# The resident tiles of an encoder kernel laid out in another order, with every large tile at a multiple of 512 bytes

## The chip, the core and the metric

The kernel runs on one core of a Trainium2 chip, in one launch. The metric is the device time of one execution in microseconds. Each core has a matrix engine (TensorE, PE in the profile, with its weight loads listed apart as PEld), a vector engine (VectorE, DVE), a scalar engine (ScalarE, ACT), a general one (GpSimd, POOL) and a queue engine (SyncE, SP). The on-chip memory SBUF has 128 partitions; a tile takes the same bytes in each partition, so its place is one number, the byte at which it starts. Matmuls read both operands from SBUF and write to PSUM.

## The reference

One layer of an encoder trunk on 1024 tokens of width 1024, all in float32:

```python
h = x
hn = rmsnorm(h, norm_mix_g)
z = hn @ w_in                               # 1024 x 2048
u, (q, k, v) = z[..., :512], split(z[..., 512:], 3)
a = pool_mixer(u, pool_w, pool_b, pool_scale)
o = chunk_attention(q, k, v, rel_bias)      # 8 heads, own chunk of 64 and 8 before it
h = h + concat([a, o]) @ w_out
hn = rmsnorm(h, norm_ffn_g)
gt, val = split(hn @ w_up, 2)               # 1024 x 2816 each
gt = causal_dwconv(gt, conv_w, conv_b)      # width 3
h = h + (gelu(gt) * val) @ w_down
gate = sigmoid(rmsnorm(h, norm_ple_g) @ w_ple_gate + b_ple_gate)
h = h + gate * (p @ w_ple)
return rmsnorm(h, final_g)
```

## The kernel before

Matmul operands are split in two parts, a rounded high one and the rest (`split`, lines 132 to 134: ScalarE writes the high part, VectorE the low one), and each product is three matmuls into one PSUM bank (`mm3`, lines 126 to 130):

```python
pe.matmul(ps, ahi, bhi, start=first, stop=False, skip_group_check=more)
pe.matmul(ps, ahi, blo, start=False, stop=False, skip_group_check=more)
pe.matmul(ps, alo, bhi, start=False, stop=last, skip_group_check=more)
```

The second operand named is the stationary one (the weights, 128 columns), the third the moving one (512 columns in most places, 256 or 320 in the attention and in the last token groups). Each matmul has a weight load of its own, which the profile shows as LDWEIGHTS under the same line.

Everything that stays on chip lies in a few large tiles, allocated once at the head of `trunk` (lines 103 to 111), which the rest of the kernel cuts up by offset. `R` (128 KiB per partition) holds operands in the matmul's number format, `F` holds plain float32 data. `ident` is the unit matrix for transposes; `vec` holds gains, biases and convolution weights by column (136 words); `small` holds statistics, counts and a column of ones (80 words). Behind these, a second region is used by one tile after another, each for a stage: `B` (attention and output projection: half of the weight ring, the probabilities, V's weights), then `V` and `TB`, `B3` (first gated products and weights of the down projection), `BQ` and `RW`, `B3T`, and `B4` (the last projection). `r(kb, n)` and `f(kb, n)` give slices of R and F at `kb` KiB; `r` with kb from 128 up goes to B.

The tiles are packed in the order in which the pool names them. The first free byte of a partition is 1152, behind 1024 bytes of DMA scratch and four constants at 32 bytes each. So the places before are

| tile | bytes | starts at | modulo 512 |
|---|---|---|---|
| R | 131072 | 1152 | 128 |
| F | 62464 | 132224 | 128 |
| ident | 512 | 194688 | 128 |
| vec | 544 | 195200 | 128 |
| small | 320 | 195744 | 160 |
| B, V, B4 | 32768, 4096, 32768 | 196064 | 480 |
| TB, B3, BQ, B3T | up to 28672 | 200160 | 480 |
| RW | 16384 | 212448 | 480 |

Nearly all operands in R and the B tiles are at multiples of 512 bytes from the start of their tile.

The stages, in order of time: norm, first projections and V (to about 50 us); attention with the other projections filled in between its steps (to about 280 us); pooling mix and output projection; then the feed-forward part. That one works on 22 blocks of 128 hidden units. `up` makes a block's two up products from seven half-size products (`step`, line 784, and `product`, line 728), whose weights are summed by GpSimd and split ahead by `prepare`, three steps before their use. The first two blocks go down by `down` (lines 861 to 876) out of `B3`. The sixteen blocks 2 to 17 go down in four groups by seven half-size products each (`down_next`, lines 980 to 994), called in between the steps of `up`; its four operand pairs lie in three quarters of `BQ` and, the fourth, at `r(60)`:

```python
spots = [B[:, 1024 * z:1024 * (z + 1)] for z in range(3)] + [r(60, 1024)]
```

The first two of them are weights, the third and the fourth moving operands. One call has 24 matmuls: four output tiles by two pairs by three. Each call then splits the next operands out of `RW`, into which SP's and GpSimd's queues load and add the stored blocks `Yd` and the weights. Blocks 18 and 19 go down out of `B3T`, in whose products one of six weight slices lies in R (again `r(60)`), the last two out of R. `ple_mm` and `gate_mm` (lines 1122 to 1134) are the last projections.

TensorE's order is written out by hand, as the code runs; the other engines are ordered by the recording layer. [...]

Of the kernel before, what the change touches and what calls it, by code (L numbers as in the profile page):

```python
# [6 lines left out]
F32 = mybir.dt.float32  # L7
# [4 lines left out]
P = 128  # L12
# [26 lines left out]
NVEC = C_GL + KT  # L39
# [54 lines left out]
def trunk(tc, xT, pT, vecs, w_qk0, w_in, w_v, bias, counts, pool_w, w_out, w_up, w_down,  # L94
# [4 lines left out]
    with tc.tile_pool(name="sb", bufs=1) as sb, \  # L99
            tc.tile_pool(name="ps", bufs=1, space=bass.MemoryType.PSUM) as pp, \  # L100
            tc.manual_schedule(engines={mybir.EngineType.PE}):

        R = sb.tile([P, 32768], F32R, name="R")
        F = sb.tile([P, 15616], F32, name="F")
        ident = sb.tile([P, P], F32, name="ident")
        vec = sb.tile([P, NVEC], F32, name="vec")
        small = sb.tile([P, 80], F32, name="small")
        PS = pp.tile([P, 8, 512], F32, name="PS")

        b_pool = tc.tile_pool(name="b1", bufs=1)  # L110
# [4 lines left out]
        def r(kb, n):  # L115
            if kb >= 128:
                return B[:, int((kb - 128) * KW):int((kb - 128) * KW) + n]
            return R[:, int(kb * KW):int(kb * KW) + n]

        def f(kb, n):  # L120
            return F[:, int(kb * KW):int(kb * KW) + n]

# [1154 lines left out]
```

## Time and profile before

| | |
|---|---|
| time, median of 3 runs | 1167.14 us (1165.75 to 1167.91) |
| span of the profiled execution | 1166.0 us |
| granted TensorE clock, mean of the span | 0.997 |
| DMA traffic | 115.93 MB, mean 99 GB/s |
| matmuls and weight loads | 5747 each |

The profile is of one execution. Its span runs from the first to the last instruction. A line of a group view gives line, engine, operation, written tile <- read tiles, shape, count, then busy time and mean of one in ns, then the engine's idle time just before them and what ended it. For PEld the names are those of the matmul that the load belongs to: "PS<-R" has both operands in R, "PS<-BQ" both in BQ, "PS<-R,BQ" one in each. A line of the order of time gives start, length, engine, line, operation and operands. Matmuls are pipelined, so their bars overlap: what one costs in a dense stretch is the distance between two starts, its pitch.

### The profile page before, as it was taken

The page shows a single profiled execution, that of the slowest core. Times are in us where ns is not written, and L with a number is a line of the kernel's source. Part 1 is how long each engine was busy: PE and PEld are TensorE (multiplying, and loading weights), DVE is VectorE, ACT ScalarE, POOL GpSimd, SP SyncE. Part 2 cuts the span into 40 slices and gives each one's busy share as a digit, 9 for nine tenths or more (in the row PEclk, how much of TensorE's full clock was granted, in tenths as well). Part 3 has the DMA queues.
Part 4 walks back from the last instruction along what each step waited for, and adds up shares of the span by engine and source line. Part 5 has one row for each costly group of instructions (what it writes and reads, how often), then busy time and mean ns, then how long its engine had stood idle before and what let it go on. Part 6 is the DMA issues. An engine that isn't in the chain of part 4 may idle for free.

```text
span 1166.0 us, 15841 instructions
## 1 busy us (share of the span) xinstructions
PE 1142.9 (98%) x5747; PEld 962.3 (83%) x5747; DVE 926.7 (79%) x1462; ACT 569.2 (49%) x991; POOL 290.1 (25%) x267
## 2 busy tenths in 40 slices
PE   9999999999999999999999999999999999999997
PEld 7988998888888778778788888887888877888897
DVE  7678877879557797889889898988898899885543
ACT  8568687665555541333343343433344345544433
POOL 0000000082003431333533353335233422120000
PEclk9999999999999999999999999999999999999999
DMA  7110102115400121544754585567556912510012
GB/s 260 37 48 30 49 12 67 40 27 182 135 27 2 55 73 38 143 127 126 167 149 127 154 176 140 128 161 167 141 133 157 207 28 91 179 47 1 1 73 73
DMA packets 58974, 115.93 MB, mean 99 GB/s; under 512 B 6672, under 2 KB 7952, under 8 KB 58896
## 3 DMA queue, kind: packets, MB, share of 16 engines
q1 hardware_dynamic: 47232, 93.88, 25.0%
q0 software_dynamic: 11520, 20.98, 11.0%
q8 instruction: 45, 0.74, 0.3%
q14 instruction: 33, 0.27, 0.1%
q10 hardware_dynamic: 144, 0.07, 0.0%
HBM read 101.79 MB, written 13.11 MB: 99 GB/s over the span
## 4 chain that ended last, share of the span: by engine, by line
PE 75%; DVE 9%; issue 7%; DMA 3%; ACT 3%; POOL 2%; SPq 0%; POOLq 0%; DVEq 0%; ACTq 0%
PE PS L129 23%; PE PS L128 23%; PE PS L130 22%; DVE R L134 3%; PE PS L367 2%; DMA RW<-Yd 1%; PE PS L384 1%; PE PS L385 1%; DMA F<-in_w_up 1%; POOL F L700 1%; POOL RW L945 1%; PE PS L342 1%; PE PS L341 1%; DVE V L805 1%; ACT R L133 1%
## 5 line engine op out<-in xcount | busy, mean ns | idle before, releaser
L128 PE MATMUL PS<-R 128*128 128x512 f32 (+1 forms) x1144 | 431.2, 377 | 8.2 <-ACT F L782 3.1
L130 PE MATMUL PS<-R 128*128 128x512 f32 (+1 forms) x1144 | 426.5, 373 | 0.9 <-DVE R L134 0.9
L129 PE MATMUL PS<-R 128*128 128x512 f32 (+1 forms) x1080 | 408.0, 378 | 0.3 <-DVE R L230 0.3
L128 PEld LDWEIGHTS PS<-R 128*128 128x128 f32 x1144 | 215.8, 189 | 47.8 <-ACT F L782 4.3
L130 PEld LDWEIGHTS PS<-R 128*128 128x128 f32 x1144 | 215.6, 188 | 40.4 <-DVE R L134 2.4
L133 ACT ACTIVATE R<-F 128x512 fp32r<-128x512 f32 (+2 forms) x217 | 136.0, 638 | 203.9 <-PE PS L129 137.1
L129 PEld LDWEIGHTS PS<-R 128*128 128x128 f32 x1080 | 203.9, 189 | 36.5 <-DVE R L230 1.1
L700 POOL TENSOR_TENSOR F<-F 128x512 f32<-128x512 f32 x88 | 154.9, 1760 | 275.2 <-DVE R L134 166.3
L134 DVE TENSOR_TENSOR R<-F,R 128x512 fp32r<-128x512 f32 (+2 forms) x213 | 171.2, 809 | 29.4 <-ACT R L133 28.3
L992 DVE TENSOR_TENSOR F<-F,PS 128x512 f32<-128x512 f32 x112 | 73.2, 678 | 8.6 <-PE PS L130 8.0
L133 ACT ACTIVATE BQ<-RW 128x512 fp32r<-128x512 f32 x72 | 42.0, 622 | 58.3 <-PE PS L129 55.2
L945 POOL DMA_DIRECT2D RW<-Yd x48 | 44.5, 927 | 102.9 <-DMA RW<-Yd 60.8
L609 ACT ACTIVATE F<-F 128x512 f32<-128x512 f32 (+1 forms) x49 | 27.9, 570 | 56.4 <-DVE F L1143 28.0
L353 ACT ACTIVATE F<-F,small 128x640 f32<-128x640 f32 (+2 forms) x64 | 44.4, 693 | 21.1 <-DVE small L351 13.0
L134 DVE TENSOR_TENSOR BQ<-RW,BQ 128x512 fp32r<-128x512 f32 x72 | 52.2, 756 | 3.1 <-PE PS L129 2.7
L375 DVE TENSOR_TENSOR B<-PS,B 128x640 fp32r<-128x640 f32 (+2 forms) x64 | 41.9, 655 | 9.9 <-ACT B L374 8.9
L819 ACT ACTIVATE F<-F,vec 128x1024 f32<-128x1024 f32 (+1 forms) x24 | 28.2, 1174 | 42.4 <-DVE F L801 41.4
L322 POOL MEMSET F<- 64x64 f32 x8 | 1.2, 152 | 183.6 <-ACT F L321 157.6
L129 PE MATMUL PS<-BQ 128*128 128x512 f32 x112 | 44.6, 398 | 1.5 <-DVE BQ L134 1.5
L129 PE MATMUL PS<-R,BQ 128*128 128x512 f32 x112 | 45.0, 402 | 0.3 <-DVE R L134 0.3
L374 ACT ACTIVATE B<-PS 128x640 fp32r<-128x640 f32 (+2 forms) x64 | 35.9, 561 | 17.7 <-PE PS L367 14.9
L130 PE MATMUL PS<-BQ 128*128 128x512 f32 x112 | 44.4, 397 | 0.0
(195 smaller groups left out, 2090.7 us busy)
## 6 DMA issues: line engine op xcount, KB each, us to landing
F<-in_w_up SPq DMA_DIRECT2D x91, 256.0 KB, 3.1
RW<-Yd SPq DMA_DIRECT2D x48, 256.0 KB, 3.6
RW<-Yd POOLq DMA_DIRECT2D x48, 256.0 KB, 5.0
RW<-in_w_down SPq DMA_DIRECT2D x40, 256.0 KB, 2.8
Yd<-F SPq DMA_DIRECT2D x34, 256.0 KB, 2.1
RW<-in_w_down POOLq DMA_DIRECT2D x32, 256.0 KB, 6.3
F<-in_w_in SPq DMA_DIRECT2D x10, 512.0 KB, 3.5
F<-in_xT SPq DMA_DIRECT2D x16, 256.0 KB, 6.0
```

What stands on the lines that cost most here:

```text
L128: pe.matmul(ps, ahi, bhi, start=first, stop=False, skip_group_check=more)
L129: pe.matmul(ps, ahi, blo, start=False, stop=False, skip_group_check=more)
L130: pe.matmul(ps, alo, bhi, start=False, stop=last, skip_group_check=more)
L133: act.activation(hi, src, AF.Copy)
L134: dve.tensor_tensor(lo, src, rv(hi), ALU.subtract)
L353: act.activation(S[:, 0:n], S[:, 0:n], AF.Exp, bias=s_[:, 0:1], scale=-1.0, accum_out=s_[:, 1:2])
L374: act.activation(hi, pst, AF.Copy)
L375: dve.tensor_tensor(lo, pst, rv(hi), ALU.subtract)
L700: pool.tensor_tensor(rawu[to], rawu[a], rawu[b], op)
L819: act.activation(y, Gb[:, 2 + a:2 + b], AF.Identity, bias=vec[:, C_CB + fi:C_CB + fi + 1], scale=cw(2))
L945: pool.dma_start(t, src, accum_op=ALU.add)
L992: dve.tensor_tensor(t, t, PS[:, 4 + d], ALU.subtract if n in (1, 5) else ALU.add)
```

## The change

The same tiles are allocated in another order, `vec` and `small` first. `small` grows by 8 words that nothing uses, `F` loses 128 words at its end that nothing uses.

```diff
+        vec = sb.tile([P, NVEC], F32, name="vec")
+        small = sb.tile([P, 88], F32, name="small")
         R = sb.tile([P, 32768], F32R, name="R")
-        F = sb.tile([P, 15616], F32, name="F")
+        F = sb.tile([P, 15488], F32, name="F")
         ident = sb.tile([P, P], F32, name="ident")
-        vec = sb.tile([P, NVEC], F32, name="vec")
-        small = sb.tile([P, 80], F32, name="small")
         PS = pp.tile([P, 8, 512], F32, name="PS")
```

`vec` then starts at 1152 and `small` at 1696, R at 2048, F at 133120, `ident` at 195072, B, V and B4 at 195584, TB, B3, BQ and B3T at 199680 and RW at 211968. From R on each is a multiple of 512. The instructions of every engine, their order and their waits are the same as before, and so are the DMAs.

## The prediction

> **What bounds the kernel now.** I read the page's head first, then the chain that ended last, then the table of stages.
>
> ```profile
> span 1166.0 us, 15841 instructions
> PE 1142.9 (98%) x5747; PEld 962.3 (83%) x5747; DVE 926.7 (79%) x1462; ACT 569.2 (49%) x991; POOL 290.1 (25%) x267
> PE 75%; DVE 9%; issue 7%; DMA 3%; ACT 3%; POOL 2%; SPq 0%; POOLq 0%; DVEq 0%; ACTq 0%
> 0.00:20.00 20.00, 17.52 (x72) 13.76 (x73) 13.74 (x24) 15.53 (x26) 0.74 (x7) 1.00 0.92 319
> ...
> 400.00:590.00 190.00, 183.83 (x795) 148.02 (x794) 160.14 (x204) 71.16 (x108) 67.84 (x48) 1.00 0.42 110
> 590.00:950.00 360.00, 358.08 (x1561) 292.24 (x1559) 316.85 (x417) 143.31 (x225) 135.64 (x110) 1.00 0.60 148
> ```
>
> TensorE is busy 98% of the span and makes 75% of the chain. In the table of stages the columns are PE, PEld, DVE, ACT, POOL, then granted clock and DMA share. Between 590 and 950 us PE is busy 358.08 of 360 us at clock 1.00, so this stage is as long as its matmuls follow each other; a nanosecond saved per matmul is saved in the end. VectorE, the next engine, is busy 316.85 of 360 (88%).
>
> A busy PE does not show how fast matmuls follow each other, because their bars overlap (0.39 us long, one every 0.23 us). The weight loads do: nothing overlaps among them when all matmuls are 512 columns wide, so busy time plus the idle time before them, less what a releaser explains, is the pitch. Weight loads, 590 to 950 us, by operands:
>
> ```profile
> L130 PEld LDWEIGHTS PS<-R 128*128 128x128 f32 x335 | 62.9, 188 | 13.1
> L128 PEld LDWEIGHTS PS<-R 128*128 128x128 f32 x334 | 62.7, 188 | 14.1 <-issue 0.8
> L129 PEld LDWEIGHTS PS<-R 128*128 128x128 f32 x334 | 62.7, 188 | 13.1
> ...
> L128 PEld LDWEIGHTS PS<-R,BQ 128*128 128x128 f32 x93 | 17.5, 188 | 4.4
> L129 PEld LDWEIGHTS PS<-BQ 128*128 128x128 f32 x93 | 17.5, 188 | 5.9 <-DVE BQ L134 2.0
> L128 PEld LDWEIGHTS PS<-BQ 128*128 128x128 f32 x93 | 17.4, 187 | 4.6
> L130 PEld LDWEIGHTS PS<-BQ 128*128 128x128 f32 x93 | 17.4, 187 | 4.1
> L129 PEld LDWEIGHTS PS<-R,BQ 128*128 128x128 f32 x92 | 17.2, 187 | 4.3
> L130 PEld LDWEIGHTS PS<-R,BQ 128*128 128x128 f32 x92 | 17.2, 187 | 3.8
> ```
>
> Products inside R: (62.9 + 13.1) / 335 = 226.9 ns. The six BQ rows: busy 104.2, idle 27.1 less 2.0 waited for VectorE, so 129.3 us over 556, 232.6 ns. The loads themselves take the same 187 to 188 ns. So a product that touches BQ costs more, and no wait on another engine explains it.
>
> The order of time shows it too (matmul starts; the first three lines are the ends of a run of 26 R matmuls, then two rounds of BQ):
>
> ```profile
> 593.80 0.39 PE L128 MATMUL PS<-R 128*128 128x512 f32 x1
> ...
> 599.47 0.39 PE L129 MATMUL PS<-R 128*128 128x512 f32 x1
> 599.69 0.39 PE L130 MATMUL PS<-R 128*128 128x512 f32 x1
> 599.92 0.40 PE L128 MATMUL PS<-BQ 128*128 128x512 f32 x1
> 600.16 0.40 PE L129 MATMUL PS<-BQ 128*128 128x512 f32 x1
> 600.39 0.40 PE L130 MATMUL PS<-BQ 128*128 128x512 f32 x1
> 600.63 0.39 PE L128 MATMUL PS<-R,BQ 128*128 128x512 f32 x1
> 600.86 0.40 PE L129 MATMUL PS<-R,BQ 128*128 128x512 f32 x1
> 601.10 0.39 PE L130 MATMUL PS<-R,BQ 128*128 128x512 f32 x1
> ...
> 602.73 0.39 PE L128 MATMUL PS<-BQ 128*128 128x512 f32 x1
> ```
>
> R: 593.80 to 599.69 is 5.89 us for 26 steps, 226.5 ns. BQ: 599.92 to 602.73 is 2.81 us for 12, 234.2 ns. I take the middle of the two measures: 226.7 inside R (226.9 and 226.5), 233.4 with BQ (232.6 and 234.2), a difference of 6.7 ns.
>
> **What the change touches.** No instruction is added, removed or moved on any engine or DMA queue, SP's and POOL's included; there is no new wait. Only bytes move. Before, R starts at byte 1152 = 2*512 + 128 of its partition and the B tiles (B, TB, B3, BQ, B3T, B4) at 196064 or 200160, both 480 past a multiple of 512. After, both start at a multiple. Two things change: the absolute place (R by 128 modulo 512, B by 32), and the distance between R and B, from 352 to 0 modulo 512.
>
> Which of the two costs the 6.7 ns? A third kind of stream decides: the down product late in the kernel, where five of six weights and all moving operands lie in B3T, and one weight in R.
>
> ```profile
> 996.21 0.39 PE L128 MATMUL PS<-B3T 128*128 128x512 f32 x1
> ...
> 1000.81 0.40 PE L130 MATMUL PS<-B3T,R 128*128 128x512 f32 x1
> ```
>
> 20 steps in 4.60 us: 230.0 ns, 3.3 over R. In the BQ rounds every weight lies in BQ, but half the moving operands in R (the pair at r(60)). If the place of B were the fault, B3T would be as slow as BQ; if it is the mix of the two distances, it should be milder, as it is. I take the mix: while one matmul streams, the next one's weights are read, and the two streams go in step only while their distance stays of one kind. After the change every distance among R and B is a multiple of 512, the kind that runs at 226.7 inside R.
>
> **The sum.**
> (1) BQ: 28 calls of down_next with 24 matmuls each, 672 matmuls by 6.7 ns: 4.5 us; by the ends of the two measures (232.6 - 226.9 and 234.2 - 226.5) 3.8 to 5.2.
> (2) The B3 and B3T down products: 96 + 96 matmuls by 3.3 ns: 0.6 us.
> (3) R matmuls right behind a B group, which have not yet come back in step:
>
> ```profile
> 289.06 0.39 PE L128 MATMUL PS<-R 128*128 128x512 f32 x1
> ...
> 291.14 0.39 PE L128 MATMUL PS<-R 128*128 128x512 f32 x1
> ```
>
> 9 steps in 2.08 us, 231.1 ns, 4.4 over R. Such groups of ten stand behind the four mixes, the four parts of the early down product, the two late ones and the eight ple products of the first token group: 18 at most, 0.8 us; I take 0.5, since some end sooner or stand behind a wait, which takes the step away by itself.
> (4) 240 matmuls with a weight ring half in B (from 60 to 280 us): by the two ends 0 and 240 * 6.7 = 1.6 us. The widths change there every few matmuls, so I take a value near nothing, 0.3. The 256-wide ones gain nothing, by the last stage:
>
> ```profile
> 1109.86 0.28 PE L128 MATMUL PS<-R 128*128 128x256 f32 x1
> ...
> 1111.90 0.28 PE L130 MATMUL PS<-R 128*128 128x256 f32 x1
> 1112.02 0.28 PE L128 MATMUL PS<-B 128*128 128x256 f32 x1
> ...
> 1112.73 0.28 PE L128 MATMUL PS<-R 128*128 128x256 f32 x1
> ```
>
> R: 17 steps in 2.04 us, 120.0 ns. B: 6 steps in 0.71, 118.3.
> (5) Other engines and DMA. ScalarE's split out of F takes 631 ns, out of RW 622, with different places modulo 64 bytes; both hide under PE, as does a load:
>
> ```profile
> L133 ACT ACTIVATE R<-F 128x512 fp32r<-128x512 f32 x84 | 53.0, 631 | 109.9 <-PE PS L129 90.0 <-issue 11.2 <-POOL F L700 7.0
> L133 ACT ACTIVATE BQ<-RW 128x512 fp32r<-128x512 f32 x59 | 34.3, 622 | 52.4 <-PE PS L129 52.4
> F<-in_w_up SPq DMA_DIRECT2D x91, 256.0 KB, 3.1
> RW<-in_w_down SPq DMA_DIRECT2D x40, 256.0 KB, 2.8
> ```
>
> I take 0. Without that cover: in the first 20 us, where DMA is at 0.92, PE idles 2.5 us, and loads 10% (0.3 of 3.1) quicker or slower would shift it by 0.25; VectorE has 12% to spare in the long stage against the 1.1% that PE gains.
> Together 4.5 + 0.6 + 0.5 + 0.3 = 5.9 us. The profiled span of 1166.0 becomes 1160.1; it lies 1.1 under the median of the runs, so the time is 1167.1 - 5.9 = 1161.2 us. Likeliest own range: from 3.8 (the low end of (1) alone, with 0.3 lost on a slower load) 3.5, to all high ends, 5.2 + 0.6 + 0.8 + 1.6 + 0.3 = 8.5: 1158.6 to 1163.6.
>
> [...]
>
> **The rivals.**
> *No change* (0.11): the 6.7 ns follow from the pattern of the products (two weight pairs in turn), not from the place, or VectorE, with 88%, takes up the slack. For it: VectorE's share, and the stage from 400 to 590 us, where PE already idles 6.2 us. Against: the R stream changes its pair just as often and keeps its pitch. Time 1167, at most 1 us off. That the change doesn't do what it says is the same case.
> *Larger gain* (0.06): even 226.9 holds a stall. From the 256-wide pitch, (226.7 - 120.0) / 256 = 0.417 ns a column, so 512 columns are 213.4 ns and 13.3 are fixed. The groups that keep shapes apart count the matmuls of that width:
>
> ```profile
> L128 PE MATMUL PS<-R 128*128 128x512 f32 x952 | 375.7, 395 | 8.2 <-ACT F L782 3.1 <-ACT V L782 2.7 <-DVE F L798 1.8
> L128 PE MATMUL PS<-R,B 128*128 128x512 f32 x80 | 33.5, 419 | 0.0
> ```
>
> Three lines of 952 and 80 each, 672 with BQ and 192 with B3 and B3T make 3960. If a start at 512 freed all of it, 3960 * 13.3 = 53 us: 1114. Against: B3T, at another absolute place, is not under R. [...] No run before shows such a pitch at 512 columns.
> *Slower* (0.12): absolute place matters the other way: with every operand at 0 modulo 512, the first line of each weight load meets the first line of a stream, and all R matmuls run like BQ's. Price: 3960 - 672 = 3288 more at 6.7 ns, 22.0 us: 1189. It decides as soon as R's pitch rises by over 1.5 ns (3960 * 1.5 = 5.9 us, what the mix gives back). For it: the cause inside the memory is not seen. Against: two starts, 128 and 480, are seen, and inside R, where weights and streams already share a remainder, nothing is slow.
>
> **How the numbers follow.** The forecast has 0.71, at 1161.2. The larger gain adds to faster: 0.77. Same 0.11, slower 0.12. 0.2% of this kernel, about what its measurement can tell, is 2.3 us; the likeliest range lies beyond it. The range takes in no change with 0.9 us of the spread of the runs, 1168.0, and goes 1 us below the low end of the sum, 1157.5: 0.71 + 0.11 lie in it, the larger gain and the slower case outside.
>
> **What would show it.** Right: BQ weight loads at 226 to 228 ns instead of 232.6, R's unchanged within 0.5; B3T at 227; the stage from 590 us about 3.7 us shorter (556 * 6.7) with PE idle still about 2 us; instruction counts equal. Wrong: BQ rows still 233 (pattern, not place); R's pitch off 226.7 either way (absolute place); pitch as forecast but longer idle before PE by VectorE or DMA (the gain taken back).

## The result, and the profile after

| | before | after |
|---|---|---|
| median of 20 runs | 1168.06 us (1164.61 to 1171.33) | 1164.99 us (1160.28 to 1168.37) |
| span of the profiled execution | 1166.0 us | 1158.5 us |
| granted TensorE clock of that execution | 0.997 | 0.997 |

The ratio of the times is 0.9969, 95% interval 0.9958 to 0.9980: 3.6 us less, between 2.3 and 4.9 (the two medians alone differ by 3.1). The forecast was 5.9 us less, 1161.2. The one profiled execution shows 7.5 us, so this pair of profiles overstates the gain by a factor of two.

The head of the page after, its chain by engine, and three rows of the table of stages (PE, PEld, DVE, ACT, POOL, then granted clock, DMA share, GB/s):

```profile
span 1158.5 us, 15841 instructions
PE 1136.7 (98%) x5747; PEld 963.0 (83%) x5747; DVE 929.2 (80%) x1462; ACT 568.6 (49%) x991; POOL 289.9 (25%) x267
PE 80%; DVE 8%; issue 5%; ACT 3%; DMA 2%; POOL 1%; SPq 0%; POOLq 0%; DVEq 0%; ACTq 0%
```
```profile
0.00:20.00 20.00, 17.90 (x73) 14.31 (x74) 14.00 (x25) 15.74 (x26) 0.73 (x7) 1.00 0.93 331
...
400.00:590.00 190.00, 184.10 (x795) 149.45 (x795) 160.72 (x205) 71.79 (x110) 67.79 (x47) 0.99 0.42 110
590.00:950.00 360.00, 358.01 (x1577) 295.51 (x1577) 323.99 (x425) 143.16 (x226) 132.81 (x110) 1.00 0.60 149
```

The instruction counts are the same on every engine. In the 360 us from 590 on, TensorE is as busy as before (358.01 against 358.08) and does 1577 matmuls instead of 1561: 16 more, which at 226.7 ns each are 3.6 us. VectorE goes from 316.85 to 323.99 busy in the same stretch (90%), since more of its work falls into it.

The weight loads of that stage, grouped by operands (count | busy, mean ns | idle before, and what ended it):

```profile
L128 PEld LDWEIGHTS PS<-R 128*128 128x128 f32 x334 | 62.7, 188 | 13.5 <-issue 0.4
L130 PEld LDWEIGHTS PS<-R 128*128 128x128 f32 x334 | 62.7, 188 | 13.1
L129 PEld LDWEIGHTS PS<-R 128*128 128x128 f32 x333 | 62.5, 188 | 12.8
L130 PEld LDWEIGHTS PS<-R,BQ 128*128 128x128 f32 x96 | 18.0, 188 | 3.7
L129 PEld LDWEIGHTS PS<-BQ 128*128 128x128 f32 x96 | 18.0, 188 | 5.8 <-DVE BQ L134 2.1
L129 PEld LDWEIGHTS PS<-R,BQ 128*128 128x128 f32 x96 | 18.0, 188 | 4.4 <-DVE R L134 0.7
L130 PEld LDWEIGHTS PS<-BQ 128*128 128x128 f32 x96 | 18.0, 188 | 3.7
L128 PEld LDWEIGHTS PS<-R,BQ 128*128 128x128 f32 x96 | 18.0, 188 | 3.7
L128 PEld LDWEIGHTS PS<-BQ 128*128 128x128 f32 x96 | 18.0, 188 | 3.7
```

R: the L130 row gives (62.7 + 13.1) / 334 = 226.9 ns, as before. The six BQ rows: 108.0 busy, 25.0 idle less 2.8 that VectorE explains, 130.2 us over 576: 226.0 ns where it was 232.6. The loads still take 188 ns each; only the time between them is gone.

The order of time after (start, length), at the three places that the prediction showed: a B group with the R matmuls behind it, a call with BQ, the late down product out of B3T:

```profile
288.34 0.39 PE L128 MATMUL PS<-R 128*128 128x512 f32 x1
...
290.38 0.39 PE L128 MATMUL PS<-R 128*128 128x512 f32 x1
...
597.08 0.39 PE L128 MATMUL PS<-BQ 128*128 128x512 f32 x1
...
602.52 0.39 PE L128 MATMUL PS<-R 128*128 128x512 f32 x1
...
988.74 0.39 PE L128 MATMUL PS<-B3T 128*128 128x512 f32 x1
...
995.54 0.39 PE L128 MATMUL PS<-B3T 128*128 128x512 f32 x1
```

Nine steps behind B in 2.04 us, 226.7 ns (231.1 before); the 24 of the call in 5.44, 226.7 (234.2); thirty of B3T in 6.80, 226.7 (230.0). All three now run like R.

The two traces, matmul by matmul: from each 512 columns wide to the next start, those pairs alone that follow without a wait (at most 260 ns), by the operands of the first:

```
operands            pairs   before   after    gained, us
BQ (with or w/o R)    668    233.5   226.7     4.5
B3                     80    230.8   226.6     0.3
B3T                    80    230.1   226.6     0.3
B, B4, late            70    231.7   227.6     0.3
R, from 280 us       2480    227.2   226.9     0.7
R,B in attention      202    232.7   230.8     0.4
R in attention        315    230.7   231.0    -0.1
256 columns, all     1158    119.3   119.5    -0.3
```

Together 6.1 us. So the matmuls gained what the sum had (5.9), and the time gained less. Where the rest went is the question of the last two experiments; those before them ask what sets the pitch.

### The profile page after: what moved, and what is told of

It reads as the page before. It is cut to its first block, busy times and chain, and to the rows that moved or that the text cites. A ratio compares the mean times of both kernels' runs of the same rounds, so it can differ in the third digit from the quotient of the medians.

```text
span 1158.5 us, 15841 instructions
## 1 busy us (share of the span) xinstructions
PE 1136.7 (98%) x5747; PEld 963.0 (83%) x5747; DVE 929.2 (80%) x1462; ACT 568.6 (49%) x991; POOL 289.9 (25%) x267
## 4 chain that ended last, share of the span: by engine, by line
PE 80%; DVE 8%; issue 5%; ACT 3%; DMA 2%; POOL 1%; SPq 0%; POOLq 0%; DVEq 0%; ACTq 0%
PE PS L128 24%; PE PS L129 24%; PE PS L130 24%; DVE R L134 3%; PE PS L367 2%; DMA F<-in_w_up 1%; PE PS L385 1%; PE PS L384 1%; POOL F L700 1%; PE PS L342 1%; PE PS L341 1%; ACT R L133 1%; DMA F<-in_w_qk 0%; DVE BQ L134 0%; DMA F<-in_w_down 0%
## 5 line engine op out<-in xcount | busy, mean ns | idle before, releaser
L130 PE MATMUL PS<-R 128*128 128x512 f32 (+1 forms) x1144 | 426.4, 373 | 0.4 <-DVE R L134 0.4
L130 PEld LDWEIGHTS PS<-R 128*128 128x128 f32 x1144 | 215.9, 189 | 39.7 <-DVE R L134 1.6
L134 DVE TENSOR_TENSOR R<-F,R 128x512 fp32r<-128x512 f32 (+2 forms) x213 | 169.5, 801 | 27.8 <-ACT R L133 26.9
L134 DVE TENSOR_TENSOR BQ<-RW,BQ 128x512 fp32r<-128x512 f32 x72 | 56.6, 818 | 2.7 <-PE PS L129 2.2
L353 ACT ACTIVATE F<-F,small 128x640 f32<-128x640 f32 (+2 forms) x64 | 44.4, 693 | 21.2 <-DVE small L351 13.1
L130 PE MATMUL PS<-BQ 128*128 128x512 f32 x112 | 43.6, 389 | 0.0
```

What stands on the lines that cost most here:

```text
L134: dve.tensor_tensor(lo, src, rv(hi), ALU.subtract)
L353: act.activation(S[:, 0:n], S[:, 0:n], AF.Exp, bias=s_[:, 0:1], scale=-1.0, accum_out=s_[:, 1:2])
```

## The experiments

Each kernel is compared with the kernel before on the same chip; the chips differ by up to 2 us in the median of before.

### What sets the pitch: a stream of nothing but matmuls

Runs of 48 (in D 96) matmuls of 512 columns follow each other; moving operands come from one tile, weights from another, both at multiples of 512, and `s` shifts the one or the other by bytes. A: constant distance between weights and moving operand. B: the moving operand alternates by threes between 0 and s. C: both shifted by the same s. D: the weights alternate by sixes.

```diff
+        def m(i, s, n=512):
+            o = 2048 * (i % 3) + s // 4
+            return M[:, o:o + n]
+        def w(i, s):
+            o = 1024 * (i % 6) + s // 4
+            return W[:, o:o + P]
+        for i in range(48):
+            pe.matmul(PS[:, i % 8], w(i, 96), m(i, 0), start=True, stop=True)
```

> Leaves the whole computation out: x is loaded and rounded into two tiles M and W, then runs of 48 matmuls of 512 columns follow each other, one run for each placement. Runs A: moving operand at a multiple of 512 bytes, weights s bytes past one, s from 0 to 480, the same all through the run. Runs B: weights at 0, moving operand in turns of three at 0 and at s. Runs C: both s past a multiple of 512. Runs D: 96 matmuls, moving at 0, weights in turns of six at 0 and at s. Theory (the distance of the two operands, when it changes along the stream, throws the weight reads out of step): all A and all C settle at 226.7 ns, or A at another constant pitch; B and D with s = 352 and s = 32 stand at 230 to 235 ns, with s = 0 at 226.7. Rival (the absolute place of an operand): C is slow for s = 32, 224 and 480, B is slow by half as much, and A is slow wherever the weights are off 512. Rival (pattern of the products): everything at 226.7. If some constant distance has a pitch well below 226.7, the 13 ns of fixed cost are a collision that a layout could avoid.

The order of time, a line for each run of 48; the next line's start less this one's, over 48, is the pitch. Distances 64, 96, 128, 160, 192, 224, 256 and 320 bytes, then from line 169 on both operands at 4, 16 and 32:

```profile
62.06 11.36 PE L129 MATMUL PS<-M,W 128*128 128x512 f32 x48
73.26 11.40 PE L131 MATMUL PS<-M,W 128*128 128x512 f32 x48
84.50 11.32 PE L133 MATMUL PS<-M,W 128*128 128x512 f32 x48
95.66 11.37 PE L135 MATMUL PS<-M,W 128*128 128x512 f32 x48
106.86 11.16 PE L137 MATMUL PS<-M,W 128*128 128x512 f32 x48
117.86 11.36 PE L139 MATMUL PS<-M,W 128*128 128x512 f32 x48
129.05 11.04 PE L141 MATMUL PS<-M,W 128*128 128x512 f32 x48
139.93 11.36 PE L143 MATMUL PS<-M,W 128*128 128x512 f32 x48
...
284.37 11.57 PE L169 MATMUL PS<-M,W 128*128 128x512 f32 x48
295.77 11.25 PE L171 MATMUL PS<-M,W 128*128 128x512 f32 x48
306.86 11.04 PE L173 MATMUL PS<-M,W 128*128 128x512 f32 x48
317.75 11.09 PE L175 MATMUL PS<-M,W 128*128 128x512 f32 x48
```

64 bytes: 11.20 us, 233.3 ns; 96: 234.2; 192: 229.2; 256: 10.88 us, 226.7. A distance that never changes costs as much as one that does, unless it is a multiple of 256. The settled pitch, from the middle of each run to the start of the next (B at 352 without that last step, which was 256 ns):

```
A  distance   0     4     16    32    64    96    128   160   192   224   256   320   352   384   448   480
   ns       226.7 232.3 233.3 233.2 233.4 234.4 232.3 233.4 228.8 233.0 226.7 233.3 234.4 232.4 228.9 233.0
B  alternating by threes, 0 and s:  0 226.7   16 232.2   32 231.1   64 232.8   96 232.8   128 232.2   256 226.7   352 232.1
C  both at s:   4 237.8   16 231.2   32, 128, 224, 480 226.7
D  weights alternating by sixes:  0 226.7   32 230.6   352 230.6
```

Three things follow. The pattern of products alone costs nothing (B and D at 0: 226.7), so the first half of the rival *no change* falls. The absolute place costs nothing at 32, 128, 224 and 480 bytes (C: 226.7 ns), so the rival *slower* and the larger gain fall for layouts like these. And "a distance that stays of one kind" is not enough: constant distances of 128 or 352 run at 232.3 and 234.4. In a stream with one constant distance, what counts is weights' start less moving operand's start modulo 256: 320, 352, 384, 448 and 480 (233.3, 234.4, 232.4, 228.9 and 233.0 ns) repeat 64, 96, 128, 192 and 224 within 0.1 ns.

A change of distance along the stream has a cost of its own. In B it is the moving operand that shifts, so `s` of 64 is a distance of 192 modulo 256: in turns with 0 it runs at 232.8, slower than either alone (228.8 and 226.7). B at 352 is the pattern of the kernel before with the sign of the distance turned round (160 modulo 256, where the kernel has 96), and gives 232.1; there the three matmuls of a turn at distance 0 take 229.8 ns on the mean and the three others 234.7. The trace of the kernel before shows the same: from one matmul inside BQ to the next, at distance 0, it takes 232.7 and 233.3 ns, so in the BQ rounds the products with the right distance are slowed too.

The runs at 226.7 and 233.3 ns differ by nothing but the place of the weights, so this place alone makes a difference of 6.6 ns a matmul to a float32r stream of this shape. By what mechanism, no run here shows.

### In the kernel: place or distance

Two versions of the kernel after. In the first everything from R on moves by 224 bytes, so that no operand is at a multiple of 512 and the distances stay. In the second R, F and `ident` stay at multiples of 512 and the B tiles move by 352, the distance before.

```diff
-        small = sb.tile([P, 88], F32, name="small")
+        small = sb.tile([P, 88], F32, name="small"); sb.tile([P, 56], F32, name="pad")
```


> The changed kernel with 224 more bytes ahead of R, so that R and every B tile stand 224 past a multiple of 512 and their distance stays a multiple of 512. Theory (distance): weight loads of BQ at 226 to 227 ns as after the change, R's the same, time as the changed kernel, 0.996 to 0.999 of before. Rival (absolute place at 512): BQ back to 232 or more, R off 226.7 too, time 1.000 of before or more.

```diff
-        ident = sb.tile([P, P], F32, name="ident")
+        ident = sb.tile([P, P], F32, name="ident"); sb.tile([P, 88], F32, name="pad")
```


> The changed kernel with 352 bytes between ident and the B tiles: R, F and ident keep their multiples of 512, the B tiles stand 352 past one, which is the distance of the kernel before. Theory (distance): BQ back at 232 to 234 ns, R 226.7, B3T near 230, time 0.999 to 1.001 of before. Rival (F's and ident's new places bring the gain, through other engines or DMA): time stays at 0.997.

On one chip, 12 runs of each and 23 of before (median 1170.00): all at 224 has 1164.86, ratio 0.9965 (0.9941 to 0.9988); B moved by 352 has 1169.06, ratio 0.9991 (0.9971 to 1.0011). The weight loads with BQ from 590 to 950 us, first with all at 224:

```profile
L130 PEld LDWEIGHTS PS<-BQ 128*128 128x128 f32 x96 | 18.0, 188 | 3.7
L128 PEld LDWEIGHTS PS<-BQ 128*128 128x128 f32 x96 | 18.0, 188 | 3.8
...
L130 PEld LDWEIGHTS PS<-R,BQ 128*128 128x128 f32 x95 | 17.8, 188 | 3.6
```

then with B moved by 352:

```profile
L128 PEld LDWEIGHTS PS<-BQ 128*128 128x128 f32 x93 | 17.4, 187 | 4.6
L130 PEld LDWEIGHTS PS<-BQ 128*128 128x128 f32 x93 | 17.4, 187 | 4.1
L129 PEld LDWEIGHTS PS<-R,BQ 128*128 128x128 f32 x92 | 17.2, 187 | 4.3
L130 PEld LDWEIGHTS PS<-R,BQ 128*128 128x128 f32 x92 | 17.2, 187 | 3.8
```

The first is the kernel after, 3.7 idle over 96 loads. The second is the kernel before to the digit: 4.6, 4.1, 4.3 and 3.8 over 93 and 92, pitch 233.2 and 233.9 in the BQ pairs of its trace; all its dense 512-wide pairs together stand at 229.09 ns, before at 229.10. So the whole gain in pitch hangs on the distance between R and the B tiles, and none of it on multiples of 512 as such. The times agree, though the interval of B moved by 352 alone leaves room for up to 3.4 us.

### Other distances, and a start at 32

One run each: the pad behind `ident` at 64, 192 and 256 bytes, and the pad ahead of R at 32.

```diff
+        ident = sb.tile([P, P], F32, name="ident"); sb.tile([P, 16], F32, name="pad")
...
+        ident = sb.tile([P, P], F32, name="ident"); sb.tile([P, 48], F32, name="pad")
...
+        ident = sb.tile([P, P], F32, name="ident"); sb.tile([P, 64], F32, name="pad")
...
+        small = sb.tile([P, 88], F32, name="small"); sb.tile([P, 8], F32, name="pad")
```

> The changed kernel with 64 bytes between ident and the B tiles, so that they stand 64 past a multiple of 512 and R at one. The table of runs says what matters is the distance modulo 256: 226.7 ns at 0 or 256, 233.4 at 64. Theory (distance modulo 256): BQ's weight loads at 231 to 234 ns on the mean of the six rows, R's at 226.7 to 227; the dense matmuls together some 5 us longer than in the changed kernel. Rival (modulo 64 or 32 is enough): BQ at 226.7, as after the change.

> The same with 192 bytes. In the table of runs a distance of 192 had the mildest pitch of the bad ones, 228.8 ns. Theory: BQ between, at 228 to 231 ns. Rival (modulo 64): 226.7.

> The same with 256 bytes. Theory (modulo 256): BQ and R at 226.7 ns, nothing to tell from the changed kernel. Rival (512 is needed, as the change's layout has it): BQ at 230 or more.

> The changed kernel with 32 more bytes ahead of R, so that R and all B tiles stand 32 past a multiple of 512, the distance staying a multiple of 512. Theory: BQ and R at 226.7 ns, the dense matmuls as in the changed kernel. Rival (a start at 64 bytes or more is needed): both slower. This run and the three before also serve as samples of the long gaps of PE: if VectorE and the transfers take part of the gain back, the gaps over 0.4 us together are longer where the pitch is 226.7 than where it is 231 and more, by about 3 us; if not, they scatter alike.

Beside one run of before (1171.11) on the same chip: distance 64 gives 1174.68, 192 1165.59, 256 1161.23, all at 32 1161.42. Single runs scatter by several us, so the pitch of the dense 512-wide pairs (some 3940 in each trace) says more: 228.95, 228.89, 227.44 and 227.42 ns, where before has 229.10 and after 227.41. A multiple of 256 is enough; a start at 32 does as well as one at 512. The BQ pairs alone: 231.6 ns at 64, 226.7 at 256, 226.8 at 32, as expected, and 232.7 at 192, where 228 to 231 were expected. Two rows of its weight loads show the miss:

```profile
L130 PEld LDWEIGHTS PS<-BQ 128*128 128x128 f32 x95 | 17.8, 188 | 4.3
L130 PEld LDWEIGHTS PS<-R,BQ 128*128 128x128 f32 x94 | 17.6, 188 | 4.3
```

Those are 232.6 and 233.0 ns. The expectation went by the constant stream at 192 (228.8); the BQ rounds alternate between 0 and 192, and that mix costs more than either, as in part B.

At a distance of 192 there was a side result: the matmuls narrower than 512 took 189.05 us in all, against 191.80 after (distances over 1.15 times the median of their width left out).

### The narrow widths

The same kind of stream, with distances for 256 and 320 columns, and 512 columns as two pieces.

```diff
+        for i in range(48):
+            pe.matmul(PS[:, i % 8, 0:256], w(i, 64), m(i, 0, 256), start=True, stop=True)
```

> Leaves the whole computation out, like the first table of runs. Runs of 48 matmuls with 256 and with 320 columns, weights s bytes past the multiple of 256 at which the moving operand stands, s in steps of 16 and 32; then 512 columns at eight more distances, and 512 columns read as two pieces of 256 with the second piece 0, 64, 128 or 192 bytes further on, at distances 0 and 192. In the kernels the narrow matmuls together took 189.0 us with the B tiles at 192, 191.8 at 0 and 191.5 at 352. Theory (the same collision, with another number of columns): the narrow pitch has a minimum at another distance than 0, near 192, 2 to 4 ns under the one at 0, and 512 columns have theirs at 0 alone. Rival (the 2.7 us came from elsewhere): narrow pitch the same at all distances or best at 0.

The order of time, 256 columns at distances 48, 64, 80 and 96:

```profile
33.75 5.82 PE L131 MATMUL PS<-M,W 128*128 128x256 f32 x48
39.41 5.61 PE L133 MATMUL PS<-M,W 128*128 128x256 f32 x48
44.85 5.86 PE L135 MATMUL PS<-M,W 128*128 128x256 f32 x48
50.55 5.87 PE L137 MATMUL PS<-M,W 128*128 128x256 f32 x48
```

At 64: 44.85 - 39.41 = 5.44 us over 48, 113.3 ns; its neighbours 117.9 (48) and 118.8 (80). The same at 192; 119.7 at 0 and between 116 and 120 elsewhere. So a best distance other than 0 was there as expected, but 6 ns under the pitch at 0 instead of 2 to 4, and at 64 too. At 320 columns all eight distances give 146.6 to 146.7. At 512 columns 240 is fast too (226.7), which part A had not tried and the expectation (0 alone) did not have. Two pieces of 256 with a gap are no faster than one of 512 (226.7 without gap and distance, 228.9 to 233.4 in the other seven).

So the widths want different distances: 512 columns 0 modulo 256 (or 240), 256 columns 64 or 192, 320 any. The attention is mostly 256 wide with one operand in R and one in the first `B`; distance 0 brought its few 512-wide products with B little (232.7 to 230.8); its products inside R stand at 231.0 too, and why both stay above 226.7 there no run shows. That gave a version that might beat both: only the attention's `B` moves by 192, and the later B tiles stay.

```diff
-        B = b_pool.__enter__().tile([P, 8192], F32R, name="B")
+        bp1 = b_pool.__enter__(); bp1.tile([P, 48], F32, name="pad"); B = bp1.tile([P, 8192], F32R, name="B")
```

> The changed kernel with the first B tile alone (the attention's) 192 bytes past a multiple of 512; V, TB, B3, BQ, B3T and B4 stay at multiples. The second table has 256 columns at 113.4 ns at a distance of 192 against 119.7 at 0, and 512 columns at 228.9 against 226.7. Theory: the 503 dense 256-wide matmuls whose moving operand lies in B go from 119.3 to about 116, as with all B tiles at 192, so 1.7 us less, and the wide ones with weights in B stay near 230.5, since their stream changes width all the time; BQ stays at 226.7. Time 0.9945 to 0.9965 of before, 1 to 2 us under the changed kernel. Rival (the attention is bound by VectorE and ScalarE, not by PE): the narrow pitch falls, PE waits longer, time as the changed kernel.

Beside it the kernel after, unchanged:

> The changed kernel on the same chip as the one with the attention's B tile at 192, for comparing their times. Theory: 0.996 to 0.998 of before, BQ at 226.7.

On one chip, 12 runs of each and 23 of before (1168.23): `B` at 192 has 1162.03, ratio 0.9951 (0.9933 to 0.9969); the kernel after, run beside it, 1166.89, ratio 0.9975 (0.9949 to 1.0001). In the traces the 256-wide pairs of the attention with B and R go from 119.4 to 115.8 ns over some 535, and all widths under 512 take 188.90 us against 191.80. The direction and the size of the dense part are as expected. The medians differ by 4.9 us where 1 to 2 were expected, and by means it is 3.0 with a 95% bound of 3.2, so by the times alone it is the best estimate and not a proven gain over after. The mean clock of the runs beside it was lower, 0.9938 against 0.9952; at equal clock the difference is 1.2 us by the fit further down.

### The kernels once more, for their waits

Both kernels unchanged, one run each.

> The changed kernel once more, for a second sample of where PE waits. If the gain of the dense matmuls (6.5 us in the first profile, against 3.6 in the times) is partly taken back by waits, this profile's gaps are longer than in the first profile of it, which was one of its fastest executions: 65 to 68 us instead of 62.2, and the gap before the next block's first product near the end of the feed-forward part is there again. If waits only scatter, it is as likely below 62 as above.

> The kernel before once more, for a second sample of where PE waits. Taken back: gaps near 63 us again or less, dense matmuls 1094 us. Scatter alone: gaps anywhere between 60 and 68.

The kernel after had 1166.75 and the kernel before 1164.95 this time, the reverse of the medians, while the pitch of the dense 512-wide pairs was the same as in the first profiles (227.44 and 229.08 ns). What differs is outside the dense stretches. The sum of all longer distances between two starts (over 1.15 times the median of their width) is 71.5 us in this profile of after and 62.2 in the first; 58.1 and 63.0 in those of before. For after 65 to 68 were expected; for before 63 or less if waits take the gain back, 60 to 68 if they only scatter. So single executions of one kernel differ by 9 us (after) and 5 us (before) with the same layout. Part of it is the clock, as the next view shows: without the stretches of 3.41 us at half clock the sums are 65.0 and 58.5, and 58.1 and 59.4. The rest is waits that come out longer or shorter.

The expectation of the start at 32 set a test for all profiles of whole kernels: the distances over 0.4 us together, longer by about 3 us where the pitch is 226.7 if VectorE and the transfers take part of the gain back. In the five profiles with before's distance or 64 or 192 they are 26.9 to 44.1 us, 33.3 on the mean; in the seven with the new distance 30.1 to 45.2, 36.0 on the mean. That is 2.7 more, inside the scatter. Without the stretches at half clock the means are 28.6 and 29.0: on the mean the waits themselves are alike, and what differs is the number of these stretches.

### Where the rest of the gain went

A wait near 389 us (for `small` from GpSimd) is equally long in both first profiles, but not equally dear. In the order of time, before:

```profile
388.92 0.39 PE L130 MATMUL PS<-R 128*128 128x512 f32 x1
391.67 0.95 PE L625 MATMUL PS<-ident,small 128*128 128x128 f32 x4 [2.36 <-POOL small L621]
...
392.84 0.63 PE L129 MATMUL PS<-R 128*128 128x512 f32 x1
393.27 0.63 PE L130 MATMUL PS<-R 128*128 128x512 f32 x1
```

and after:

```profile
387.94 0.39 PE L130 MATMUL PS<-R 128*128 128x512 f32 x1
390.67 0.65 PE L625 MATMUL PS<-ident,small 128*128 128x128 f32 x4 [2.35 <-POOL small L621]
...
391.39 0.39 PE L129 MATMUL PS<-R 128*128 128x512 f32 x1
391.62 0.40 PE L130 MATMUL PS<-R 128*128 128x512 f32 x1
```

Before, the matmuls behind it come 0.43 us apart, after 0.23. The granted clock tells why: in both first profiles it is 1.00 or 0.50, and the one stretch at 0.50 ahead of the end lasts 3.41 us (from 391.88 us on before, from 573.81 on after). In windows of that length, before, then after (columns as in the table of stages):

```profile
388.47:391.88 3.41, 1.05 (x6) 0.59 (x5) 2.71 (x5) 2.25 (x4) 3.08 (x2) 1.00 0.03 7
391.88:395.30 3.42, 3.42 (x11) 2.84 (x10) 1.35 (x3) 1.23 (x2) 0.00 (x0) 0.50 0.68 226
```
```profile
386.17:389.59 3.42, 2.15 (x10) 1.46 (x8) 2.72 (x5) 2.13 (x4) 2.13 (x3) 1.00 0.10 37
389.59:393.00 3.41, 2.33 (x12) 2.00 (x13) 1.95 (x4) 1.88 (x4) 1.03 (x1) 1.00 0.54 165
```

Before, the wait lies in one window, and the next is granted 0.50. After, the same wait falls across a boundary and costs nothing more (this execution has its half window elsewhere, from 573.81 us on). Over the twelve profiles of whole kernels the idle time in a window tells without exception whether the next one is at half clock: I took the idle time of TensorE in each window up to the last waits of the kernel (a distance over 0.3 us between two starts, less 0.23):

```
windows with 2.05 to 2.70 us idle:   24, the next one at half clock in all 24
windows with 2.04 us idle or less: 3970, the next one at half clock in none
nearest to the bound:                2.046 (half), 2.038 (full)
```

By estimate a half window costs up to 1.7 us, half of its 3.41. The windows stand on a fixed grid in both first profiles: the two stretches at half clock start 771.41 us apart before (391.88 and 1163.29), 226 times 3.41333, and 580.27 apart after (573.81 and 1154.08), 170 times. The grid has another phase in each execution (a window starts 2.76 us behind the start of the span before, 0.37 after), and 5 to 10 waits of 1.3 to 3 us stand in each, most of them at the same places of the kernel (near 389, 425, 488, 510, 574, 691, 809, 946 and 983 us), so each execution draws its number of half windows: 0 to 4 ahead of the end in the profiles of kernels with before's distance or 64 or 192, 1 to 5 in those with the new one.

The granted clock stands beside every run, so the layouts can be compared at equal clock. Over the 94 runs of the two series with rounds on one chip each (before 46, B moved by 352 12, after and all at 224 24, `B` at 192 12), a fit of the time by chip, layout and clock gives, with 95% bounds:

```
after's distances against before's, at equal clock   -5.8 us (+- 1.0)
B moved by 352                                       +0.3    (+- 1.3)
attention's B at 192                                 -7.0    (+- 1.3)
0.001 of mean clock                                   1.29   (+- 0.21)
mean clock: before's distances 0.9962 (58 runs), new ones 0.9946 (36 runs), difference 0.0016 (+- 0.0009)
```

At equal clock the new layout gains 5.8 us, what the dense matmuls gained in the traces. It runs at a mean clock lower by 0.0016, which is 1.6 * 1.29 = 2.1 us, about one half window more per execution. 5.8 - 2.1 = 3.7 us, near the 3.6 of the result; the same fit without the clock gives 3.5 (+- 1.6) for these runs. This is a fit made afterwards and no experiment. That the clock is lower is measured in these two series; the 20 runs of after in the result stand at 0.9956, only 0.0006 under 0.9962, and the clocks of the runs of before beside them are not on record, so how much of the result's own shortfall is the clock is not shown. *Why* it is lower is open. That a faster TensorE waits longer for VectorE and GpSimd at the same places, and so passes 2.05 us more often, would fit, but the profiles do not show it: the wait near 570 us was 1.8, 1.8 and 1.9 us long in three profiles with before's distance and 2.8, 1.7 and 2.6 in three of after, but from under 1.3 to 3.0 in the four others with the new distance, and under 1.3 and 2.4 at 192 and 64. No version that shortens these waits was run.

## Why the prediction was right, and where not

**The bound.** "This stage is as long as its matmuls follow each other" held from 590 to 950 us: 16 more matmuls in the same 360 us. The step that failed is the one behind it, "a nanosecond saved per matmul is saved in the end". 6.1 us were saved in matmuls and 3.6 in the time. The rival *no change* named VectorE at 88% as what could take the gain back; what the runs with rounds show is a lower granted clock, 2.1 us by the fit, behind waits outside the dense stretches. Whether VectorE's lateness is what lengthens those is the open part.

**Term 1, BQ:** 672 by 6.7 ns, 4.5 us. Measured 6.8 (233.5 to 226.7), 4.5 us.

**Term 2, B3 and B3T:** 0.6 at 3.3 ns; measured 4.2 and 3.5 over 160 pairs, 0.6.

**Term 3, R behind B:** 0.5; R from 280 us on gained 0.7, and the B groups themselves and the last projection's B4, which had no term, 0.3.

**Term 4, the attention's ring:** 0.3 of 0 to 1.6; measured 0.4 over 202 pairs, given back by 0.1 in R.

**Term 5 and the 256-wide ones:** ScalarE's split into BQ still takes 622 ns, and TensorE's busy time in the first 20 us differs by less (17.52 to 17.90) than in two executions of the kernel before (17.52 and 18.21). "The 256-wide ones gain nothing" held (a loss of 0.3); that they gain nothing from any layout would be wrong, as 64 and 192 show.

**The mechanism.** The choice between place and distance was right: all at 224 keeps the gain, B moved by 352 loses it. The reason put for it, streams that "go in step only while their distance stays of one kind", is half of it at best: a mix does cost more than its two distances alone (0 and 192: 232.7 in BQ), but a constant distance is slow as well (234.4 at 352), and 512 is not the unit but 256 (226.7 at 256). That it led to the right layout and the right sum was luck: inside R and inside each B tile the distances are multiples of 512, so the only wrong distance in the kernel was also the only mixed one. By that reason a constant shift of all weights, by 64 bytes say, would have been free; by part A it costs 6.7 ns (233.4 against 226.7) on a 512-wide matmul.

**The rivals.** *Slower* (absolute place) and *larger gain* fell with part C and with the starts at 32 and 224: 226.7 ns is the floor in every layout tried. The 13.3 ns of fixed cost came from a 256-wide pitch of 120.0 that was itself not at its best: with the 113.3 at 64 and 192 the same sum, (226.7 - 113.3) / 256 = 0.443 ns a column, makes 226.8 of 512 columns, and by this estimate nothing fixed is left to free.

**The size.** 1164.99 lies inside the range and 1.4 us above the likeliest range of its own. 0.9 us of that is the start of the sum, 1167.1 from three runs, where 20 runs give before 1168.06; for the rest the lower clock is the likely reason, as far as the fit goes.

## What to carry to other kernels

Lay all tiles that feed one matmul stream so that weights and moving operands start at the same place modulo 256 bytes when it streams 512 columns (float32r here: 226.7 ns, against 228.8 to 234.4 at every other distance tried but 240), and at a start that ran at 226.7 here (0, 32, 128, 224 or 480 bytes past a multiple of 512; 4 and 16 ran at 237.8 and 231.2); do not mix distances in one stream (0 and 192 in turns 232.8, alone 226.7 and 228.8); and measure the other widths apart: 256 columns ran best at distances of 64 and 192 (113.3 ns against 116 to 120), 320 alike at all eight (146.6 to 146.7). Put small odd-sized tiles ahead of the large ones or behind all of them, since one column of statistics shifts everything behind it. When a gain of some tenths of a per cent is read from profiles, compare the pitch of dense stretches, and read the times beside their granted clock.

## What the runs showed of the hardware that was not expected

- The pitch of a dense stream of 512-wide float32r matmuls, each with its own weight load and all at one distance, depends on the weights' start less the moving operand's start modulo 256 bytes: 226.7 ns at 0 and 240, 228.8 at 192, 230 to 234.4 at the others that were tried. With 256 columns the best are 64 and 192 (113.3 against 116 to 120), with 320 all are alike (146.6 to 146.7).
- A stream that alternates between two distances can be slower than with either alone: 0 and 192 in turns 232.7 to 232.8, where 0 has 226.7 and 192 has 228.8.
- Operands that both start 4 or 16 bytes past a multiple of 512 are slow although their distance is 0 (237.8 and 231.2 ns); at 32, 128, 224 and 480 bytes the start makes no difference (226.7).
- A window of 3.41 us in which TensorE idles 2.05 us or more is followed by one at half clock in 24 of 24 cases in twelve profiles, one with 2.04 us or less in none of 3970; the wait of 2.35 us near 389 us that falls across a window's boundary in the kernel after is followed by none.
